# Attention inside a decoder layer: unscaled probabilities, and one multiplication of each value output by reciprocal row sums that travel through DRAM

## The chip, the cores and the metric

The kernel runs on one core of one Trainium2 chip. The metric is the device time of one execution in microseconds (us); the kernel before has a median of 2579.94 us over three runs (2579.6, 2579.94 and 2585.3 us).

A core has five engines with a queue each, and every queue is worked off in order: PE (matrix products, with PEld for its weight loads), DVE (vector work), ACT (activations and casts), POOL (vector work that can't reach PSUM) and SP, which here only issues DMA transfers. An instruction waits on semaphores of other engines or of DMA transfers, and all that stands behind it on its queue waits with it.

## The reference, cut to what matters

One decoder layer on a sequence of 2048 positions and 1024 channels: a projection, three groups of mixing heads beside each other (mLSTM, attention, spatial gating), an output projection, and a feed-forward part with a convolution. The change is in the attention: 8 heads of 64 channels, causal, with a cumulated log-forget bias `F`.

```python
def forgetting_attention(q, k, v, f_pre):
    F = jnp.cumsum(jax.nn.log_sigmoid(f_pre.astype(jnp.float32)), axis=-1)
    ...
        logits = (jnp.einsum('bhtd,bhsd->bhts', qb, kb) * scale
                  + F[:, :, lo:hi, None] - F[:, :, None, :hi])
        logits = jnp.where(mask, logits, -jnp.inf)
        p = jax.nn.softmax(logits, axis=-1)
        outs.append(jnp.einsum('bhts,bhsd->bhtd', p.astype(v.dtype), vb))
```

The softmax divides each row of exponentials by its sum. The product with the values is linear in the row, so the division can stand on the probabilities or on the output.

## The kernel before, in words

**Stages.** From 0 to about 700 us the kernel computes the projection, the mLSTM and the gating; from 700 to 1117 us the attention (the first two blocks of scores of head 0 run ahead, from 660 us); then the output projection, and from about 1290 us the feed-forward part.

**Tiling of the attention.** A phase is a head `h` and a block `tb` of 512 queries, written (h, tb) below. The order of the phases is (0,1), (0,0), (0,2), (0,3), then tb = 0, 1, 2, 3 for each of the heads 1 to 6, and 2, 3, 0, 1 for head 7 (`TBS`). `scores` makes the phase's four rows of 128 queries: `q` (split in two parts that sit above each other) times `kk` into PSUM tile `sp` (line 206, the mask by line 210), DVE adds the bias `nf`, finds the row minimum `nm` and writes `L` to SBUF (line 212), ACT takes the exponential in place and sums the row into `rs` (line 223). Then POOL adds the two partial sums where a row has two parts of up to 1024 keys (line 225), takes the power -1 (line 226), and multiplies the row in place by it (line 228).

`finish` takes the phase's rows one phase later: for each block `j` of 128 keys PE transposes the four row pieces into `tp` (line 259), ACT casts them to `phi` (line 262), DVE makes the rest `plo` (line 263), and PE multiplies both with the values `vv` into `op` (lines 245 and 246). `op` is a single PSUM buffer. After the last `j`, ACT copies it to `yo` (line 250), and two DMAs write the halves of `yo` to `yt_d` and `y2_d` in DRAM (line 252).

`phase` interleaves the scores of one block with the finish of the block before. `load_q` (line 173) fetches the queries a phase ahead into four buffers, `load_k` (lines 157 and 158) and `load_v` (line 163) the next head's keys, bias and values.

**What follows.** During the last two heads `load_w` fetches the output weights into three `ld` buffers and splits them (ACT line 131, POOL or DVE line 132), and `y_load` (lines 298 and 302) reads `yt_d` and `y2_d` back. The first block of the output projection is tb = 2. The casts of what was read (`yhl`, line 131) stand on ACT between the casts of the attention. The output products are lines 54 to 56 on `wps`.

**What sets the order.** Outside a few stretches written out by hand, a list scheduler with a cost model orders each queue and assigns buffers; the program order is its priority. All DMAs of this part are issued from SP.

Of the kernel before, what the change touches and what calls it, by code (L numbers as in the profile page):

```python
# [8 lines left out]
F32 = mybir.dt.float32  # L9
F32R = mybir.dt.float32r  # L10
BF16 = mybir.dt.bfloat16
AF = mybir.ActivationFunctionType
ALU = mybir.AluOpType
# [4 lines left out]
P = 128  # L18
S = 2048
D = 1024  # L20
DFF = 2816
NH = 8
EPS = 1e-6
NEG = -1.0e30
TB = 512
# [8 lines left out]
def trunk(  # L34
# [7 lines left out]
    V, A, G, T = nc.vector, nc.scalar, nc.gpsimd, nc.tensor  # L42
    dma = nc.sync.dma_start
# [15 lines left out]
    dr = ctx.enter_context(tc.tile_pool(name="dr", bufs=1, space=DRAM))  # L59
# [13 lines left out]
    gt_d = dr.tile([2, D], F32, name="gt_d")  # L73
    hc_d = dr.tile([7, 4, P, 2, 512], F32, name="hc_d")
    act_d = dr.tile([DFF, S], F32, name="act_d")


    ident = cst.tile([P, P], F32, name="ident")
# [3 lines left out]
    mone = cst.tile([P, 1], F32, name="mone")  # L82
# [42 lines left out]
    pool, pp = Mem(), Mem(PSUM)  # L125
# [10 lines left out]


    def attention_open_right():
        pool.open("att_s", "right", ("nm", 8, 6), ("rs", 8, 6), ("even", 128, 1))
        pool.open("att_r", "right", ("kvA", 8192, 3), ("LA", 4096, 8), ("qA", 2048, 6))  # L140
        pp.open("att_r", "right", ("sp", 4096, 2))

    def attention_open_left():
        pool.open(
            "att_l", "left", ("kvB", 8192, 6), ("LB", 4096, 12), ("L2", 2048, 4), ("phl", 2048, 8), ("qB", 2048, 4), ("yo", 2048, 2),
        )
        pp.open("att_l", "left", ("tp", 2048, 3), ("op", 2048, 1))

# [33 lines left out]
    def l_tile(h, tb, c, w):  # L182
        if h and (tb == 0 or (tb, c) == (2, 1)) or (h, tb, c) == (0, 2, 1):
            tag = "L2"
        else:
            n_l[0] += 1
            tag = "LA" if h < NH - 2 and (n_l[0] - 1) % 20 < 8 else "LB"
        return pool.tile([P, w], F32, name="L", tag=tag)

    def scores(h, tb, q2, rows):  # L190

        kk, nf, _ = kv[h]
        for i in range(4):
            n_s = (tb * 4 + i + 1) * P
            parts = [(s0, min(1024, n_s - s0)) for s0 in range(0, n_s, 1024)]
            qs = slice(i * P, (i + 1) * P)

            nm = pool.tile([P, 2], F32, name="nm", tag="nm")
            L = []
            for c, (s0, w) in enumerate(parts):  # L200
                sp = pp.tile([P, 1024], F32, name="sp", tag="sp")
                for b in range(0, w, 512):
                    bw = min(512, w - b)
                    last = s0 + b + bw == n_s
                    for n in range(2):
                        T.matmul(  # L206
                            sp[:, b : b + bw], q2[n][:, qs], kk[:, s0 + b : s0 + b + bw], start=n == 0, stop=n == 1 and not last
                        )
                    if last:
                        T.matmul(sp[:, w - P : w], identb, maskb, start=False, stop=True)  # L210
                L.append(l_tile(h, tb, c, w))
                V.tensor_tensor_reduce(  # L212
                    out=L[c], in0=sp[:, :w], in1=nf[:, s0 : s0 + w], scale=-1.0, scalar=3.0e38 if c == 0 else nm[:, 0:1],
                    op0=ALU.add, op1=ALU.min, accum_out=nm[:, c : c + 1],
                )
                yield
            rows.append(L)
            rs = pool.tile([P, 2], F32, name="rs", tag="rs")

            def exps(L=L, nm=nm, rs=rs):  # L220
                n = len(L)
                for c in range(n):
                    A.activation(L[c], L[c], AF.Exp, bias=nm[:, n - 1 : n], scale=-1.0, accum_out=rs[:, c : c + 1])  # L223
                if n == 2:
                    G.tensor_tensor(rs[:, 0:1], rs[:, 0:1], rs[:, 1:2], op=ALU.add)
                G.tensor_tensor(rs[:, 0:1], rs[:, 0:1], mone, op=ALU.pow)
                for t in L:
                    G.tensor_scalar(t, t, rs[:, 0:1], 1.0, op0=ALU.mult, op1=ALU.mult)  # L228

            exps()  # L230

    behind = []

    def finish(h, tb, rows):

        ns = (tb + 1) * 4
        vv = kv[h][2]

        got = []

        def product(j, c0, hi, lo):
            if j == 0:
                got.append(pp.tile([P, 512], F32, name="op", tag="op"))
            op = got[0]
            T.matmul(op[:, c0:], vv[:, j, :], hi[:, c0:], start=(j == 0), stop=False)  # L245
            T.matmul(op[:, c0:], vv[:, j, :], lo[:, c0:], start=False, stop=(j == ns - 1))  # L246
            if j == ns - 1:
                yo = pool.tile([P, 512], F32, name="yo", tag="yo")

                A.copy(yo, op)  # L250
                for n, d in enumerate((yt_d, y2_d)):
                    dma(d[h * 64 : h * 64 + 64, tb * TB : (tb + 1) * TB], yo[64 * n : 64 * n + 64])

        for j in range(ns):
            i0 = max(0, j - tb * 4)
            c0 = i0 * P
            tp = pp.tile([P, 512], F32, name="tp", tag="tp")
            for i in range(i0, 4):
                T.transpose(tp[:, i * P : (i + 1) * P], rows[i][j // 8][:, (j % 8) * P : (j % 8 + 1) * P], ident)  # L259
            hi = pool.tile([P, 512], F32R, name="phi", tag="phl")  # L260
            lo = pool.tile([P, 512], F32R, name="plo", tag="phl")
            A.copy(hi[:, c0:], tp[:, c0:])  # L262
            V.tensor_tensor(lo[:, c0:], tp[:, c0:], hi[:, c0:].bitcast(F32), op=ALU.subtract)  # L263
            behind.append(lambda j=j, c0=c0, hi=hi, lo=lo: product(j, c0, hi, lo))
            if len(behind) > 3:
                behind.pop(0)()
            yield

    def phase(now, then, lead=0):

        rows = []
        sc, n_sc = iter(()), 0
        if now:
            sc, n_sc = scores(*now, kv.pop(now) if now in kv else load_q(*now, "qB"), rows), (4, 4, 8, 8)[now[1]]
            if now in order and now != order[-1]:
                nxt = order[order.index(now) + 1]
                kv[nxt] = load_q(*nxt, "qB")
        n_fin = sum(4 * (t[1] + 1) for t in then)
        fin = (u for t in then for u in finish(*t))
        done = 0  # L280
        for n in range(n_sc):
            next(sc)
            while done < (n + 1 - lead) * (n_fin - 5) // (n_sc - lead):
                next(fin)
                done += 1
        for _ in sc:
            pass
        for _ in fin:
            pass
        return now and [(*now, rows)]  # L290
# [985 lines left out]
    for n, (half, i) in enumerate(steps):  # L1276
# [5 lines left out]
        if n == len(steps) - 1:  # L1282
            while background:
                if next(background[0], True):
                    background.pop(0)
            n_accs[0] = 2
            pool.close("proj_r")
            pp.close("proj_r")
            attention_open_right()

            load_k(0)
            first_rows = [], []
            first = [scores(0, tb, load_q(0, tb, "qA"), r) for tb, r in zip((1, 0), first_rows)]
            load_v(0, (0, 1))
            background += first
# [25 lines left out]
    for f in first:  # L1321
        for _ in f:
            pass
    attention_open_left()
    load_v(0, (2, 3))
    last = [(0, 1, first_rows[0]), (0, 0, first_rows[1])]
# [742 lines left out]
```

## Time and profile before

| | us |
|---|---|
| median of three runs | 2579.94 |
| the profiled execution | 2583.37 |
| its span in the trace | 2581.6 |
| attention, 701 to 1117 us | 416 |
| PE busy in it | 404.25 |
| DVE, ACT, POOL busy in it | 357.00, 338.90, 245.12 |
| matmul clock granted, mean of the span | 0.997 |

The views are those of one profiled execution. A group row names line, engine, operation, out<-in with shapes and the count, then busy us and mean ns of one, then the idle time before these instructions and what ended it. A row of waits names who waited for whom, the total in us, the number of times and the longest. A row of a timeline has the start, the length, the engine, the line and the operation; neighbours of one kind are merged, so the length of an "x4" row holds all four and the waits between them. Idle time of an engine that is not the bottleneck costs nothing, and a busy PE is not a PE at its peak, since its products are pipelined.

### The profile page before, as it was taken

How to read it: one execution, taken by the hardware profiler on the slowest of the kernel's cores; microseconds unless marked ns; L12 is line 12 of the kernel's file. 1: busy time of each engine (PE TensorE's matmuls, PEld its weight loads, DVE VectorE, ACT ScalarE, POOL GpSimd, SP SyncE). 2: the span in 40 equal slices, each digit the busy share in tenths (PEclk: the TensorE clock that was granted, in tenths of full speed). 3: DMA queues.
4: the chain of work that ended last, by engine and by line, in shares of the span. 5: the costliest groups of instructions: out<-in, count | busy, mean ns of one | idle time of the engine just before them, and what ended most of it. 6: DMA issues, size and time to landing. Idle time of an engine off the chain costs nothing.

```text
span 2581.6 us, 36385 instructions
## 1 busy us (share of the span) xinstructions
PE 2531.6 (98%) x12569; PEld 2099.5 (81%) x12569; DVE 1994.3 (77%) x3406; ACT 1282.8 (50%) x2443; POOL 405.2 (16%) x537
## 2 busy tenths in 40 slices
PE   7999999999999999999999999999999999999999
PEld 6888888888787877778878888888888888788787
DVE  7667656576388889865689888888888887897797
ACT  5433353433388888844455454444444444444443
POOL 2013310133266556510000000000000000000000
PEclk9999999999999999999999999999999999999999
DMA  7335753454654445266823222264222218567523
GB/s 260 116 119 168 222 173 101 133 160 139 177 158 128 123 127 168 56 200 230 285 82 106 84 80 83 89 233 158 82 82 86 78 67 293 178 207 249 188 90 123
DMA packets 302672, 379.58 MB, mean 147 GB/s; under 512 B 31758, under 2 KB 194412, under 8 KB 300440
## 3 DMA queue, kind: packets, MB, share of 16 engines
q1 hardware_dynamic: 302488, 377.26, 46.5%
q8 instruction: 99, 1.62, 0.3%
q14 instruction: 85, 0.70, 0.1%
HBM read 276.44 MB, written 100.74 MB: 146 GB/s over the span
## 4 chain that ended last, share of the span: by engine, by line
PE 49%; DVE 9%; DMA 5%; ACT 3%; issue 2%; POOL 1%; SPq 0%; DVEq 0%; ACTq 0%; POOLq 0%
PE ub L55 10%; PE ub L54 10%; PE ub L56 10%; PE db L55 3%; PE db L56 3%; PE db L54 3%; DVE wspl L1668 2%; PE tp L259 2%; PE sp L206 2%; DMA wd<-in_w_down_dram 2%; PE op L245 1%; PE op L246 1%; ACT L L223 1%; DVE L L212 1%; DMA hc_d<-hl 1%
## 5 line engine op out<-in xcount | busy, mean ns | idle before, releaser
L54 PE MATMUL acc<-wh,hh 128*128 128x512 f32 (+2 forms) x752 | 281.7, 375 | 1.2 <-DVE vhl L815 1.2
L54 PE MATMUL ub<-T,wsph 128*128 128x512 f32 x704 | 273.9, 389 | 1.2 <-ACT wsph L1529 1.2
L55 PE MATMUL ub<-T,wsph 128*128 128x512 f32 x704 | 274.3, 390 | 0.2 <-DVE T L1477 0.2
L56 PE MATMUL ub<-T,wspl 128*128 128x512 f32 x704 | 273.9, 389 | 0.0
L55 PE MATMUL acc<-wl,hh 128*128 128x512 f32 (+2 forms) x752 | 270.5, 361 | 0.6 <-DVE wl L648 0.6
L56 PE MATMUL acc<-wh,hl 128*128 128x512 f32 (+2 forms) x752 | 270.7, 362 | 0.3 <-DVE hl L606 0.2
L55 PE MATMUL db<-wspl,wsph 128*128 128x512 f32 x616 | 241.5, 392 | 4.4 <-DVE wspl L1668 4.1
L56 PE MATMUL db<-wsph,wspl 128*128 128x512 f32 x616 | 239.8, 389 | 0.0
L54 PE MATMUL db<-wsph 128*128 128x512 f32 x616 | 239.7, 389 | 0.0
L1529 ACT CAST wsph<-S 128x512 fp32r<-128x512 f32 x176 | 109.3, 622 | 219.5 <-PE ub L55 152.0
L263 DVE TENSOR_TENSOR plo<-tp,phi 128x512 fp32r<-128x512 f32 (+1 forms) x320 | 187.1, 607 | 30.7 <-ACT phi L262 28.5
L55 PE MATMUL ub<-B,wsph 128*128 128x512 f32 x528 | 205.7, 390 | 1.0 <-DVE B L1477 0.9
L54 PE MATMUL ub<-B,wsph 128*128 128x512 f32 x528 | 205.7, 390 | 0.0
L56 PE MATMUL ub<-B,wspl 128*128 128x512 f32 x528 | 205.4, 389 | 0.0
L223 ACT ACTIVATE L<-L,nm 128x1024 f32<-128x1024 f32 (+2 forms) x192 | 172.5, 903 | 34.5 <-DVE nm L212 32.7
L259 PE MATMUL tp<-ident,L 128*128 128x128 f32 x1088 | 177.3, 274 | 4.7 <-DVE plo L263 2.3
L262 ACT CAST phi<-tp 128x512 fp32r<-128x512 f32 (+1 forms) x320 | 160.0, 521 | 42.0 <-PE tp L259 40.3
L1667 ACT CAST wsph<-act 128x512 fp32r<-128x512 f32 x132 | 82.3, 624 | 195.7 <-PE db L55 187.9
L206 PE MATMUL sp<-kk,q 128*128 128x512 f32 (+3 forms) x640 | 169.3, 375 | 3.3 <-DVE nm L212 2.2
L228 POOL TENSOR_SCALAR L<-L,rs 128x1024 f32<-128x1024 f32 (+2 forms) x192 | 167.7, 884 | 11.0
L56 PEld LDWEIGHTS acc<-wh,hl 128*128 128x128 f32 x752 | 143.1, 191 | 22.4 <-DVE hl L606 0.9
L55 PEld LDWEIGHTS acc<-wl,hh 128*128 128x128 f32 x752 | 143.7, 191 | 20.5 <-DVE wl L648 1.8
(339 smaller groups left out, 5975.0 us busy)
## 6 DMA issues: line engine op xcount, KB each, us to landing
w<-in_w_up_dram SPq DMA_DIRECT2D x88, 512.0 KB
wd<-in_w_down_dram SPq DMA_DIRECT2D x176, 256.0 KB
wa<-in_w_ada_dram SPq DMA_DIRECT2D x96, 256.0 KB
act_d<-yc SPq DMA_DIRECT2D x44, 512.0 KB
act<-act_d SPq DMA_DIRECT2D x44, 512.0 KB
wr<-in_w_in_dram SPq DMA_DIRECT2D x64, 256.0 KB
q<-q_d SPq DMA_DIRECT2D x128, 128.0 KB
hc_d<-hl SPq DMA_DIRECT2D x28, 512.0 KB
```

The lines of the kernel that those rows point to most:

```text
L54: T.matmul(ps, lh, rh, start=start, stop=False, skip_group_check=resume)
L55: T.matmul(ps, lh, rl, start=False, stop=False, skip_group_check=resume)
L56: T.matmul(ps, ll, rh, start=False, stop=stop, skip_group_check=resume)
L206: T.matmul(sp[:, b : b + bw], q2[n][:, qs], kk[:, s0 + b : s0 + b + bw], start=n == 0, stop=n == 1 and not last)
L223: A.activation(L[c], L[c], AF.Exp, bias=nm[:, n - 1 : n], scale=-1.0, accum_out=rs[:, c : c + 1])
L228: G.tensor_scalar(t, t, rs[:, 0:1], 1.0, op0=ALU.mult, op1=ALU.mult)
L259: T.transpose(tp[:, i * P : (i + 1) * P], rows[i][j // 8][:, (j % 8) * P : (j % 8 + 1) * P], ident)
L262: A.copy(hi[:, c0:], tp[:, c0:])
L263: V.tensor_tensor(lo[:, c0:], tp[:, c0:], hi[:, c0:].bitcast(F32), op=ALU.subtract)
L1529: A.copy(self.wa[p][0], self.source(p))
L1667: A.copy(hi, v)
L1668: V.tensor_tensor(lo, v, hi.bitcast(F32), op=ALU.subtract)
```

## The change

The exponentials are no longer multiplied by POOL. The row sums of a phase's four rows go into one tile `rs` of 128 x 2 x 4; after the fourth row POOL adds the two halves and takes the power -1 for the four rows at once, and a DMA writes the 512 reciprocals, element by element, to a row of a new DRAM tensor `r_d`. When the phase's `op` has been copied to `yo`, a DMA reads that row back into all 128 partitions (`rb`, in the ring of `yo`, which now has four buffers), POOL multiplies `yo` by it, and only then the two halves are written. `rs` has five buffers of 32 bytes where it had six of 8, and an unused tile shrinks by as much, so that later addresses stay the same.

```diff
+    r_d = dr.tile([NH, S], F32, name="r_d")
...
-        pool.open("att_s", "right", ("nm", 8, 6), ("rs", 8, 6), ("even", 128, 1))
+        pool.open("att_s", "right", ("nm", 8, 6), ("rs", 32, 5), ("even", 16, 1))
...
-            ... ("qB", 2048, 4), ("yo", 2048, 2),
+            ... ("qB", 2048, 4), ("yo", 2048, 4),
...
     def scores(h, tb, q2, rows):
         kk, nf, _ = kv[h]
+        rs = pool.tile([P, 2, 4], F32, name="rs", tag="rs")
...
             rows.append(L)
-            rs = pool.tile([P, 2], F32, name="rs", tag="rs")
-
-            def exps(L=L, nm=nm, rs=rs):
-                n = len(L)
-                for c in range(n):
-                    A.activation(L[c], L[c], AF.Exp, bias=nm[:, n - 1 : n], scale=-1.0, accum_out=rs[:, c : c + 1])
-                if n == 2:
-                    G.tensor_tensor(rs[:, 0:1], rs[:, 0:1], rs[:, 1:2], op=ALU.add)
-                G.tensor_tensor(rs[:, 0:1], rs[:, 0:1], mone, op=ALU.pow)
-                for t in L:
-                    G.tensor_scalar(t, t, rs[:, 0:1], 1.0, op0=ALU.mult, op1=ALU.mult)
-
-            exps()
+            n = len(L)
+            for c in range(n):
+                A.activation(L[c], L[c], AF.Exp, bias=nm[:, n - 1 : n], scale=-1.0, accum_out=rs[:, c, i : i + 1])
+        if n == 2:
+            G.tensor_tensor(rs[:, 0, :], rs[:, 0, :], rs[:, 1, :], op=ALU.add)
+        G.tensor_tensor(rs[:, 0, :], rs[:, 0, :], mone.broadcast_to([P, 4]), op=ALU.pow)
+        dma(r_d[h, tb * TB : (tb + 1) * TB].rearrange("(i p) -> p i", p=P), rs[:, 0, :])
...
                 A.copy(yo, op)
+                rb = pool.tile([P, 512], F32, name="rb", tag="yo")
+                dma(rb, r_d[h : h + 1, tb * TB : (tb + 1) * TB].broadcast_to([P, TB]))
+                G.tensor_tensor(yo, yo, rb, op=ALU.mult)
                 for n, d in enumerate((yt_d, y2_d)):
                     dma(d[h * 64 : h * 64 + 64, tb * TB : (tb + 1) * TB], yo[64 * n : 64 * n + 64])
```

The scheduler orders the queues anew. Line numbers in the rows of the change are those of the changed kernel.

POOL's queue at head 1, in the kernel before: the end of the phase with tb = 1 and the start of the one with tb = 2 (`rs` the sums, `mone` the constant -1).

```order
L226 TENSOR_TENSOR rs<-rs,mone 128x1
L228 TENSOR_SCALAR L<-L,rs 128x896
L226 TENSOR_TENSOR rs<-rs,mone 128x1
L228 TENSOR_SCALAR L<-L,rs 128x1024
L225 TENSOR_TENSOR rs<-rs 128x1
L226 TENSOR_TENSOR rs<-rs,mone 128x1
L228 TENSOR_SCALAR L<-L,rs 128x1024
```

The same queue in the changed kernel, a whole head:

```order
L249 TENSOR_TENSOR yo<-yo,rb 128x512
L225 TENSOR_TENSOR rs<-rs,mone 128x4
L249 TENSOR_TENSOR yo<-yo,rb 128x512 x2
L224 TENSOR_TENSOR rs<-rs 128x4
L225 TENSOR_TENSOR rs<-rs,mone 128x4
L249 TENSOR_TENSOR yo<-yo,rb 128x512
L224 TENSOR_TENSOR rs<-rs 128x4
L225 TENSOR_TENSOR rs<-rs,mone 128x4 x2
```

A row's multiplications are gone, and four rows share one power. On PE the order stays as it was from phase (1,2) to the start of head 6 (some 17 of the 32 phases); it moves in small pieces before and after.

SP's queue at the start of the attention, before: the outputs of (0,1) and (0,0), and between and behind them the queries of (1,0) and (1,1).

```order
L252 DMA yt_d<-yo 64x512
L252 DMA y_d<-yo 64x512
L163 DMA vv<-v_d 128x4x128 x2
L173 DMA q<-q_d 64x512 x4
L252 DMA yt_d<-yo 64x512
L252 DMA y_d<-yo 64x512
L157 DMA kk<-k_d 64x2048
L173 DMA q<-q_d 64x512 x4
```

The same place in the changed kernel, from the store of (0,2)'s sums to that of (0,3)'s and the query part behind it:

```order
L226 DMA r_d<-rs 128x4x1
L164 DMA vv<-v_d 128x4x128
L248 DMA rb<-r_d 128x512
L164 DMA vv<-v_d 128x4x128 x3
L251 DMA yt_d<-yo 64x512
L251 DMA y_d<-yo 64x512
L174 DMA q<-q_d 64x512 x4
L248 DMA rb<-r_d 128x512
L158 DMA kk<-k_d 64x2048
L251 DMA yt_d<-yo 64x512
L251 DMA y_d<-yo 64x512
L174 DMA q<-q_d 64x512 x3
L226 DMA r_d<-rs 128x4x1
L174 DMA q<-q_d 64x512
```

The queries of (1,1) stood behind the write of (0,0); now three of their four parts also stand behind the load of `rb` for (0,0), and the fourth behind the store of (0,3)'s sums.

SP's queue near the end of the attention, before: the write of (7,2) and the reading back of block tb = 2 for the output projection.

```order
L252 DMA yt_d<-yo 64x512
L252 DMA y_d<-yo 64x512
L298 DMA ld<-yt_d 128x512
L302 DMA ld<-y_d 128x512
L298 DMA ld<-yt_d 128x512 x5
```

In the changed kernel, there:

```order
L226 DMA r_d<-rs 128x4x1 x2
L248 DMA rb<-r_d 128x512
L251 DMA yt_d<-yo 64x512
L251 DMA y_d<-yo 64x512
L297 DMA ld<-yt_d 128x512
L301 DMA ld<-y_d 128x512
L297 DMA ld<-yt_d 128x512 x5
```

The load of `rb` for (7,2) now stands behind the stores of two later phases' sums, (7,3) and (7,0), and in front of the write that the reading back waits for.

ACT's queue at that time, in phase (7,1), before: the casts of the attention (`phi`) and those of the blocks read back (`yhl`).

```order
L223 ACTIVATE L,rs<-L,nm 128x640
L262 CAST phi<-tp 128x512 x6
L131 CAST yhl<-ld 128x512
L262 CAST phi<-tp 128x512
L131 CAST yhl<-ld 128x512
L262 CAST phi<-tp 128x512 x2
L131 CAST yhl<-ld 128x512
```

In the changed kernel:

```order
L222 ACTIVATE L,rs<-L,nm 128x640
L261 CAST phi<-tp 128x512 x9
L132 CAST yhl<-ld 128x512
L261 CAST phi<-tp 128x384
L132 CAST yhl<-ld 128x512
L261 CAST phi<-tp 128x256
L261 CAST phi<-tp 128x128
L132 CAST yhl<-ld 128x512
```

The first cast of a block read back stands behind nine casts of the attention where it stood behind six, and the next ones follow it closer.

2 lines of the change are left out of this document (1 added, 1 removed).

## The prediction

> **What bounds the kernel now.** I read the page's busy times first, then the attention alone in the windows view, since every edit lies there.
>
> ```profile
> PE 2531.6 (98%) x12569; PEld 2099.5 (81%) x12569; DVE 1994.3 (77%) x3406; ACT 1282.8 (50%) x2443; POOL 405.2 (16%) x537
> 701.00:1117.00 416.00, 404.25 (x2473) 327.27 (x2472) 357.00 (x708) 338.90 (x737) 245.12 (x372) 1.00 0.47 128
> ```
>
> The second row lists PE, PEld, DVE, ACT and POOL busy, then the granted clock. In the 416 us of attention PE is busy for 404.25 us, at a clock of 1.00. It idles for 11.75 us, and POOL's 245.12 us lie beside that. Then the waits of PE and of its weight loader in the same stretch:
>
> ```profile
> PE op L245 <- ACT yo L250: 4.3, 13, 0.8
> PE tp L259 <- DVE plo L263: 2.3, 5, 0.7
> PE tp L259 <- POOL L L228: 1.2, 2, 1.0
> PEld tp L259 <- POOL L L228: 3.9, 8, 1.2
> PEld tp L259 <- POOL rs L226: 1.1, 1, 1.1
> ```
>
> PE's largest named wait is for the one `op` buffer, which the change leaves as it is. POOL ends 1.2 us of PE's idle time in 2 places and 5.0 us of the loader's in 9. The loader works ahead of PE, so part of its 5.0 us costs nothing. Last, the chain of waits over the attention, by line (the row ends there):
>
> ```profile
> by line: PE tp L259 11.4%; PE sp L206 10.5%; PE op L245 7.2%; issue 6.7%; PE op L246 6.5%; ACT L L223 4.6%; DVE L L212 4.6%; POOL L L228 3.3%; DVE plo L263 3.2%; ACT phi L262 2.8%; POOL rs L226 1.7%; DMA ld<-in_w_out_dram 1.4%; DMA ld<-yt_d
> ```
>
> POOL has 3.3% and 1.7%, thus 20.8 us of 416. This counts every step at which POOL came last before something, also where PE had other products meanwhile; the waits of PE itself are the better price, and the chain's share is kept for a rival.
>
> **What is taken out.** POOL's groups in the attention:
>
> ```profile
> L228 POOL TENSOR_SCALAR L<-L,rs 128x1024 f32<-128x1024 f32 (+4 forms) x184 | 161.8, 890 | 10.4
> L226 POOL TENSOR_TENSOR rs<-rs,mone 128x1 f32<-128x1 f32 x120 | 66.5, 557 | 77.6 <-ACT L L223 72.6
> L225 POOL TENSOR_TENSOR rs<-rs 128x1 f32<-128x1 f32 x64 | 13.5, 211 | 94.4 <-ACT L L223 94.3
> L132 POOL TENSOR_TENSOR wo0l<-ld,wo0h 128x512 fp32r<-128x512 f32 x4 | 5.2, 1290 | 6.9 <-ACT wo0h L131 6.9
> ```
>
> The multiplications go (161.8 us), and of the powers and sums three in four: 30 of the 120 powers stay (16.7 us), 16 of the 64 sums (3.4 us), if four columns cost what one does. New on POOL are 32 multiplications of 128x512; the last row is the same operation at the same size, 1.29 us, thus 41.3 us. POOL's 241.8 us fall to about 61 us. None of this is path by itself. ACT's exponentials and DVE's rows keep their number and size. What PE gains is that a row is ready after ACT instead of after ACT and POOL. The price is between 1.2 us (PE's idle time alone) and 6.2 us (the loader's too). I take 3.5, near the middle, since the loader's longest waits stand where PE waits too:
>
> ```profile
> 1107.63 0.33 PE L259 MATMUL tp<-ident,L 128*128 128x128 f32 x1 [0.97 <-POOL L L228]
> 1109.36 0.33 PE L259 MATMUL tp<-ident,L 128*128 128x128 f32 x1 [0.23 <-POOL L L228]
> ```
>
> These two are all of PE's 1.2 us, in the last phase. In the middle heads PE's order is unchanged, so nothing is to be had there but such waits.
>
> POOL also splits half of the first output weights, between its row multiplications. One wait there falls on ACT, which is on the path of the casts:
>
> ```profile
> ACT wo0h L131 <- DMA ld<-in_w_out_dram: 2.3, 2, 2.1
> ```
>
> A freer POOL gives the `ld` buffers back sooner. Between 0 and 2.3 us; I take 1, since the wait is ACT's and not PE's.
>
> **What is added, on the queues.** 64 DMAs (a store and a load in each phase) on SP, which has room. What counts is what stands behind their waits. A load that waits for a store of this part shows what a pass through DRAM takes:
>
> ```profile
> 1087.37 0.46 SPq L252 DMA_DIRECT2D yt_d<-yo  x1
> 1087.88 0.59 SPq L252 DMA_DIRECT2D y_d<-yo  x1
> 1089.68 0.33 SPq L298 DMA_DIRECT2D ld<-yt_d  x1
> 1090.33 0.33 SPq L302 DMA_DIRECT2D ld<-y_d  x1
> ```
>
> From the issue of `y_d` to that of its reader 2.45 us; I take 2.4 for a landing. The write of `yo` now waits for `rb` (2.4) and POOL (1.29), wherever `rb` is not early.
>
> Middle heads: the store of (h,1)'s sums and the loads of `rb` for (h,0) and (h,1) stand ahead of the queries of (h+1,0). Head 3 in the trace of before:
>
> ```profile
> 857.53 0.55 POOL L226 TENSOR_TENSOR rs<-rs,mone 128x1 f32<-128x1 f32 x1
> 865.82 2.46 SPq L173 DMA_DIRECT2D q<-q_d  x4
> 883.40 0.33 PE L206 MATMUL sp<-kk,q 128*128 128x128 f32 x2
> ```
>
> The sums of (3,1) are ready at 858.1, and the queries fetched at 865.8 are first used at 883.4. From the store on: landing x, `rb` 2.4, POOL 1.29, two writes 1.06, the last query part 0.59 and 1.8 to land, together 7.1 + x. This reaches 883.4 only if x is over 18 us. With x near 2.4 it costs 0; the cover is the 15 us by which the queries are early.
>
> Start: here the cover is thin. Queries of (1,1):
>
> ```profile
> 719.24 2.43 SPq L173 DMA_DIRECT2D q<-q_d  x4
> 726.08 2.46 SPq L173 DMA_DIRECT2D q<-q_d  x4
> 730.68 0.55 POOL L226 TENSOR_TENSOR rs<-rs,mone 128x1 f32<-128x1 f32 x1
> 733.21 0.69 PE L206 MATMUL sp<-kk,q 128*128 128x512 f32 x3
> ```
>
> They were issued at 726.1 and used at 733.2. Now the fourth part stands behind the store of (0,3)'s sums, whose power ends at 731.2: store 0.35, part 0.59, landing 1.8, so 734 against 733.2. I take 1 us of loss, between 0 (PE finds other products) and 2.
>
> End: `rb` of (7,2) stands behind the store of (7,0)'s sums. In before, their last power is here:
>
> ```profile
> 1087.02 0.55 POOL L226 TENSOR_TENSOR rs<-rs,mone 128x1 f32<-128x1 f32 x1
> 1095.62 0.62 ACT L131 CAST yhl<-ld 128x512 fp32r<-128x512 f32 x1 [1.69 <-DMA ld<-yt_d]
> 1098.45 0.62 ACT L131 CAST yhl<-ld 128x512 fp32r<-128x512 f32 x1 [0.23 <-DMA ld<-yt_d]
> 1100.23 0.62 ACT L131 CAST yhl<-ld 128x512 fp32r<-128x512 f32 x1 [0.51 <-DMA ld<-yt_d]
> ```
>
> Without the multiplications between, that power ends at about 1087.0; store 0.35, `rb` 0.4 after it, landing at 1089.7, POOL until 1091.0, the write 3.7 us later than at 1087.4. So the reading back is 3.7 us later, and ACT, which waited 1.69 us there, stands before it after three more casts of some 0.8 us (2.4 us). That leaves 1.69 + 3.7 - 2.4 = 3.0, which is 1.3 more, and the next two waits grow since fewer casts lie between: 2.5 us in all, between 0 (the output products already between the attention's fill PE) and 6.2 (3.7 and 2.5).
>
> **The sum.** -3.5 - 1 + 1 + 2.5 = -1 us. The bounds are -6.2 - 2.3 = -8.5 and -1.2 + 2 + 6.2 = +7. Against the profiled execution (2583.37, of which 1.8 lie outside its span) this is 2582.4. The median of the runs, 2579.94, lies 3.4 below that execution, so the forecast for the median is 2579, and from 2571.4 to 2587 by the bounds. 0.3% of 2580 is 7.7 us, about what a measurement of this kernel can tell from no change; nearly all of this lies inside it.
>
> **The rivals.** First, **slower, by the store of the sums**. It writes 512 separate elements of 4 bytes, and no row of before has such a store. Nearest is a load in 1024 pieces of 64 bytes:
>
> ```profile
> 15.45 0.39 SPq L1086 DMA_DIRECT2D gw<-in_w_in_dram  x1
> 20.79 0.58 POOL L1159 COPY wr<-gw 128x16 f32<-128x16 f32 x2 [5.98 <-DMA gw<-in_w_in_dram]
> ```
>
> 5.3 us from issue to use, which is under the 18 us of the middle heads. Above 18 us it decides: then SP stands before the write of (h,1), and the queries of each next head come late by what is over. At 20 us that is 2 us for each of 7 heads, +14, so 2593. For it: the path has four steps in series on one in-order queue, and nothing measures the first. Against it: a load of twice as many pieces takes 5.3. The Trainium skill speaks for this rival: "DMA: Bandwidth & Descriptors", section Rules for kernel authors, says that an access whose last dimension is not contiguous becomes one descriptor per element, and its Specifications say that under 512 bytes the engine reads, modifies and writes. No run shown here has a 4-byte store; by that rule x lies above a full-size landing, by how much the page doesn't say.
>
> Second, **faster, by the chain**. If each of POOL's steps in the chain is PE's own time, 20.8 us go instead of 3.5, which with the other terms gives -18.3, so 2562. For it: DVE and ACT are 86% and 81% busy here, so a row that is ready earlier may also spare waits that carry another engine's name. Against it: PE idles for 11.75 us in all, and only 1.2 of them end on POOL.
>
> **How the numbers follow.** No measurable change 0.54, the slow store 0.27, the chain 0.19. The predicted time is 2579. The likeliest case's own range is 2571 to 2587; cases of both signs hold nearly half, so the range goes on to 2566 and 2597, leaving out the farther half of the chain's gain and a store beyond 20 us. Faster by over 0.3% 0.19, within 0.54, slower 0.27.
>
> **What would show it.** Right: in 701 to 1117 us POOL's busy time near 65 us, no wait of `tp` for POOL, PE busy for some 404 us in a stretch as long as before; a short wait of PE near the first scores of (1,1); longer waits of ACT's `yhl` casts for `ld` between 1093 and 1105 us. Wrong: SP waiting at the write of `yo` past the time when queries are due, in every head; PE waiting for `sp`'s queries in the middle heads; or PE's waits for DVE and ACT falling by many us, which the orders don't explain.

## The result, and the profile after

The changed kernel takes 2710.34 us (median of four runs, 2704.91 to 2716.79) against 2579.77 of the kernel before on the same chip: a ratio of 1.0501, 95% interval 1.0489 to 1.0513. It is slower by 5%, some 130 us, where 2579 was forecast and 2597 was the upper end of the range.

Busy times of the page of the changed kernel, then its attention in the windows view (it now ends near 1231 us; PE, PEld, DVE, ACT and POOL busy, granted clock, DMA share, GB/s):

```profile
PE 2574.9 (95%) x12553; PEld 2123.1 (78%) x12569; DVE 1992.7 (73%) x3406; ACT 1285.1 (47%) x2443; POOL 231.5 (9%) x233
701.00:1231.00 530.00, 437.26 (x2499) 353.46 (x2499) 355.51 (x706) 341.48 (x737) 78.18 (x81) 0.91 0.53 115
```

POOL's work in the attention fell from 245 to 78 us, as the change means it to. But for about the same number of products (2499, before 2473) the stretch is 530 us long instead of 416. PE is idle for 93 us of it, where it was idle for 12, and busy for 33 us more, since the granted clock is 0.91 where it was 1.00. The waits of PE and of SP from 701 to 1250 us (total, times, longest):

```profile
PE sp L208 <- DMA q<-q_d: 46.4, 19, 7.0
PE tp L258 <- DVE plo L262: 23.2, 3, 8.6
PE sp L208 <- DVE nm L214: 20.2, 6, 9.7
...
SPq L251 <- POOL yo L249: 176.4, 20, 11.3
SPq L251 <- POOL rs L224: 63.1, 11, 10.5
SPq L226 <- POOL rs L225: 40.7, 14, 5.2
```

PE's largest wait is one that it did not have: for the queries. SP, which fetches them, stands for some 240 us before the writes of `yo` (line 251), because POOL's multiplication is not done. In the kernel before it stood there for 147 us (701 to 1117 us, for ACT), and no query was late for it. Why POOL is late shows in one stretch of a middle head, first SP's and POOL's queues, then PE's:

```profile
922.82 0.59 SPq L248 DMA_DIRECT2D rb<-r_d  x1
930.07 0.53 SPq L226 DMA_DIRECT2D r_d<-rs  x1
930.64 1.56 SPq L248 DMA_DIRECT2D rb<-r_d  x1
940.37 0.45 SPq L251 DMA_DIRECT2D yt_d<-yo  x1
941.56 2.47 SPq L174 DMA_DIRECT2D q<-q_d  x4
...
926.91 1.28 POOL L249 TENSOR_TENSOR yo<-yo,rb 128x512 f32<-128x512 f32 x1 [5.27 <-DMA rb<-r_d]
939.06 1.29 POOL L249 TENSOR_TENSOR yo<-yo,rb 128x512 f32<-128x512 f32 x1 [9.62 <-DMA rb<-r_d]
...
945.43 0.77 PE L208 MATMUL sp<-kk,q 128*128 128x512 f32 x1 [3.85 <-DMA q<-q_d]
```

The load of `rb` issued at 922.82, with no store just ahead of it, is there for POOL 4.1 us later. The one issued at 930.64, right behind a store of the sums, is there after 8.4. SP can't write before that, and only then fetches the queries, at 941.56; PE runs out of other work at that moment. For the most part the queries themselves are not slow here (median 3.6 us from issue to landing in this stage, upper quartile 4.9; 3.2 and 3.8 before): they are issued late. The same stretch in the windows view (columns as above):

```profile
936.00:941.00 5.00, 4.94 (x32) 3.65 (x30) 3.67 (x11) 4.69 (x12) 1.86 (x3) 1.00 0.00 0
941.00:945.00 4.00, 0.59 (x4) 0.21 (x2) 1.83 (x7) 1.02 (x4) 0.59 (x1) 0.86 0.63 161
945.00:950.00 5.00, 2.86 (x10) 2.24 (x11) 0.00 (x0) 0.28 (x1) 0.00 (x0) 0.50 1.07 219
952.00:957.00 5.00, 4.88 (x33) 4.05 (x32) 4.25 (x8) 4.00 (x9) 0.10 (x1) 1.00 0.84 143
```

After PE's gap the granted clock is 0.50 for several us, and a product of 128x512 with the queries takes 0.77 us (945.43, above) where a like one takes 0.40 at a clock of 1.00:

```profile
954.11 0.40 PE L208 MATMUL sp<-kk,q 128*128 128x512 f32 x1
```

So the wait costs more than its own length. The Trainium skill, "TensorE: Matmul & The Clock Gate", section Part 1: The HAM clock gate, says that the clock goes to half after an idle window of about 3.4 us. Here less was enough: by the trace's clock records it fell at 943.9 us, 2.3 us into this gap, and it also fell behind gaps of 1.9 and 2.1 us (before 781.98 and 843.66 us). The measurement decides.

### The profile page after: what moved, and what is told of

Its sections match the earlier page's. It is cut to its first block, busy times and chain, and to the rows that moved or that the text cites. A ratio compares the mean times of both kernels' runs of the same rounds, so it can differ in the third digit from the quotient of the medians.

```text
span 2715.1 us, 36025 instructions
## 1 busy us (share of the span) xinstructions
PE 2574.9 (95%) x12553; PEld 2123.1 (78%) x12569; DVE 1992.7 (73%) x3406; ACT 1285.1 (47%) x2443; POOL 231.5 (9%) x233
## 5 line engine op out<-in xcount | busy, mean ns | idle before, releaser
L54 PE MATMUL ub<-T,wsph 128*128 128x512 f32 x704 | 277.0, 394 | 1.2 <-ACT wsph L1528 1.2
L55 PE MATMUL ub<-T,wsph 128*128 128x512 f32 x704 | 277.3, 394 | 0.2 <-DVE T L1476 0.2
L208 PE MATMUL sp<-kk,q 128*128 128x512 f32 (+3 forms) x640 | 181.8, 396 | 69.3 <-DMA q<-q_d 46.4
L258 PE MATMUL tp<-ident,L 128*128 128x128 f32 x1088 | 185.2, 286 | 23.4 <-DVE plo L262 23.2
L208 PEld LDWEIGHTS sp<-kk,q 128*128 128x128 f32 x640 | 119.7, 201 | 101.8 <-issue 34.4
L258 PEld LDWEIGHTS tp<-ident,L 128*128 128x128 f32 x1088 | 138.8, 148 | 52.0 <-DVE plo L262 18.2
L214 DVE CUSTOM_DVE_ANT_0 L<-sp,nf 128x1024 f32<-128x1024 f32 (+7 forms) x128 | 126.0, 987 | 57.4 <-PE sp L208 24.1
```

What stands on the lines that cost most here:

```text
L54: T.matmul(ps, lh, rh, start=start, stop=False, skip_group_check=resume)
L55: T.matmul(ps, lh, rl, start=False, stop=False, skip_group_check=resume)
L208: T.matmul(sp[:, b : b + bw], q2[n][:, qs], kk[:, s0 + b : s0 + b + bw], start=n == 0, stop=n == 1 and not last)
L214: V.tensor_tensor_reduce(out=L[c], in0=sp[:, :w], in1=nf[:, s0 : s0 + w], scale=-1.0, scalar=3.0e38 if c == 0 else nm[:, 0:1], op0=ALU.add ...
```

## The experiments

Each kernel was compared with the kernel before on the same chip, and ratios are to that. "Lag" below is how far a kernel's profiled execution stands behind that of the kernel before at the same DVE instruction, worked out by pairing the DVE rows of both traces. The profiled execution of before is itself 3.4 us over its median and lost most of that ahead of 737 us, so from there on a lag of -3 means no difference (`before_shift`, which alters no order and has its effect behind the attention, shows -3.0).

| us of the kernel before | 641 | 737 | 770 | 965 | 1032 | 1180 | 1295 | 2150 |
|---|---|---|---|---|---|---|---|---|
| the change | 1.9 | 20.5 | 30.6 | 69.6 | 92.1 | 123.4 | 122.0 | 135.6 |
| `neither`: no store, no load | 0.2 | -2.8 | -3.2 | -5.3 | -6.2 | -7.6 | -8.3 | 5.3 |
| `store_only` | 0.4 | 15.2 | 17.8 | 44.1 | 61.0 | 74.8 | 74.6 | 88.2 |
| `load_only` | 0.1 | 2.8 | 3.1 | 0.8 | 12.1 | 22.3 | 18.7 | 31.5 |
| `neither_addr`: the same, addresses kept | -0.6 | -2.2 | -2.7 | -4.7 | -3.9 | -5.2 | -7.8 | -9.3 |
| `before_shift`: before, addresses moved | -0.1 | -3.0 | -3.0 | -3.0 | -2.2 | -2.3 | -1.9 | 11.2 |
| `fix_poolq`: 16 bytes, POOL's queue | -0.9 | -2.8 | -3.2 | -5.5 | 1.6 | 23.9 | 18.0 | 17.0 |
| `hybrid`: the same in heads 0 to 4 | -0.9 | -1.2 | -1.6 | -3.8 | 4.9 | 5.8 | 6.1 | 5.1 |
| `early_sp`: 16 bytes, SP, early load | 0.5 | -0.2 | -0.7 | -3.0 | -1.2 | 0.5 | -0.8 | -1.4 |

**Which part costs it.** Four kernels take the change apart. `neither`, from the change:

```diff
-        dma(r_d[h, tb * TB : (tb + 1) * TB].rearrange("(i p) -> p i", p=P), rs[:, 0, :])
...
-                rb = pool.tile([P, 512], F32, name="rb", tag="yo")
-                dma(rb, r_d[h : h + 1, tb * TB : (tb + 1) * TB].broadcast_to([P, TB]))
-                G.tensor_tensor(yo, yo, rb, op=ALU.mult)
```

> Without the store of the sums, the load of rb and POOL's multiplication by it: the division by the row sums is left out, POOL's row multiplications stay away. My theory (the 130 us come from the round trip of the sums on SP's in-order queue): all of them are gone, 2580 within 8 us, PE idle some 12 us in the attention. Rival, POOL's row work was part of the path before: below 2570, down to 2562. Rival, the loss comes from the new order of PE, ACT and DVE that goes with the change: above 2650 still.

`store_only` takes out the last three of these lines and keeps the store.

> Only the store of the sums, nothing reads them (the multiplication of yo and the load of rb are left out, so the outputs stay undivided). My theory (the stores cost by what waits for them, the loads of rb behind them and SP behind those): 2580 to 2600, since no instruction on SP waits for a store and the queries have some 15 us to spare. Rival, 16384 elements of 4 bytes take the DMA engines or the DRAM from everything else: above 2650, queries late in every head all the same.

`load_only` takes out the store, keeps the three, and fills `r_d` once at the start:

```diff
+    dma(r_d.rearrange("h (a b) -> (h a) b", b=P), ones)
```

> The sums are not stored (r_d holds ones, written once at the start; the division is left out), rb is loaded and multiplied as in the change. My theory: rb lands some 2.5 to 4 us after its issue instead of 8 to 9, SP is held for some 5 us a phase instead of 10 to 12, and the queries are in time in most heads: 2585 to 2625. Rival, any round trip ahead of the write of yo on SP is enough: above 2650, with PE waiting for q in every head.

`store_16b`:

```diff
-        dma(r_d[h, tb * TB : (tb + 1) * TB].rearrange("(i p) -> p i", p=P), rs[:, 0, :])
+        dma(r_d[h, tb * TB : (tb + 1) * TB].rearrange("(p i) -> p i", p=P), rs[:, 0, :])
```

> As the change, but each partition writes its four reciprocals as one piece of 16 bytes, 128 pieces instead of 512 (the reciprocals reach the wrong queries). My theory, landing goes by the number of pieces: some 4 us instead of 8.5, and 2600 to 2640. Rival, the time is in something that a store of 128 partitions has whatever its pieces: landing 8 us or more and above 2680.

| run | median, us | ratio, 95% interval |
|---|---|---|
| `neither` | 2586.69 | 1.0025, 1.0016 to 1.0035 |
| `store_only` | 2671.55 | 1.0351, 1.0334 to 1.0369 |
| `load_only` | 2614.81 | 1.0129, 1.0114 to 1.0144 |
| `store_16b` | 2611.87 | 1.0119, 1.0104 to 1.0134 |

The DMAs, with the multiplication that waits for them, are the loss: without them 0.25% is left. `neither` alone does not clear the new order of the queues, for in it DVE and ACT work in the order of the kernel before (all but one of DVE's 3406 instructions). `store_16b` does: all queues work in the order of the change there (PE's as far as its records go, of which some are missing), and it is 98 us faster than the change. My expectation for the store alone was wrong, though. Nothing reads the sums in `store_only`, and still it costs 3.26 points over `neither`, 84 us; load and multiplication alone cost 1.04 points, 27 us, and both together 12 us more than their sum. Waits of PE, then of SP, in `store_only`:

```profile
PE sp L208 <- DMA q<-q_d: 36.1, 13, 7.2
PE sp L208 <- DVE nm L214: 10.4, 3, 10.0
...
SPq L174 <- DMA nf<-nf_d: 25.3, 5, 6.7
...
SPq L174 <- DMA kk<-k_d: 21.1, 7, 5.6
```

SP now stands for 46 us before the queries until other loads have landed, keys and bias, where it does so for 0.5 us in `store_far64` (below). So the store delays transfers that have nothing to do with it. With pieces of 16 bytes it costs nothing that can be measured over `load_only`, and the 12 us that come only with both are gone too.

**Where the 13 us of the feed-forward are from.** `neither` is 8.3 us ahead at 1295 us and 5.3 behind at 2150, in a stage that the change doesn't touch. The groups of one product there, first the kernel before, then `neither`, then `neither_addr` (below):

```profile
L54 PE MATMUL ub<-T,wsph 128*128 128x512 f32 x704 | 273.9, 389 | 1.2 <-ACT wsph L1529 1.2
...
L54 PE MATMUL ub<-T,wsph 128*128 128x512 f32 x701 | 275.8, 394 | 1.2 <-ACT wsph L1524 1.2
...
L54 PE MATMUL ub<-T,wsph 128*128 128x512 f32 x704 | 273.9, 389 | 1.2 <-ACT wsph L1524 1.2
```

Each product takes 394 ns instead of 389, with the same order on PE. What is said ahead of the prediction, that the unused tile shrinks so that later addresses stay the same, is not so: in the compiled programs the tiles behind it lie 128 bytes higher (the first `wsph` buffer at 155232 instead of 155104). Three kernels test that. `neither_addr` and `after_addr`, from `neither` and from the change:

```diff
-        pool.open("att_s", "right", ("nm", 8, 6), ("rs", 32, 5), ("even", 16, 1))
+        pool.open("att_s", "right", ("nm", 8, 6), ("rs", 32, 5), ("even", 160, 1))
```

and `before_shift`, from the kernel before:

```diff
-        pool.open("att_s", "right", ("nm", 8, 6), ("rs", 8, 6), ("even", 128, 1))
+        pool.open("att_s", "right", ("nm", 8, 6), ("rs", 8, 6))
```

> As the run without store, load and multiplication (2586.7), but with the unused tile at 160 bytes instead of 16, so that all tiles behind it lie at the addresses of the kernel before (in the change they lie 128 bytes higher). Theory: the 13 us that the feed-forward lost there, at the same order of products and a clock of 1.00, come from the addresses: 2574, from 2570 to 2578. Rival, they come from anything else that the change alters ahead of the feed-forward: 2587 again.

> The kernel before without its unused tile of 128 bytes, so that all tiles behind it lie 128 bytes higher, where the change has them. Theory of the addresses: 2592, from 2588 to 2597, lost between 1390 and 2150 us. Rival, the addresses don't matter: 2580.

> The change with its unused tile at 160 bytes, so that the tiles behind it lie at the addresses of the kernel before; nothing else. Theory, the addresses are a term of their own, some 13 us beside the DMAs: 2694 to 2701. Rival, they matter only where PE is never idle, or not here: 2706 and above.

| run | median, us | ratio, 95% interval |
|---|---|---|
| `neither_addr` | 2573.64 | 0.9967, 0.9955 to 0.9978 |
| `before_shift` | 2594.75 | 1.0047, 1.0032 to 1.0062 |
| `after_addr` | 2695.08 | 1.0443, 1.0429 to 1.0457 |

All three came as the theory had them. The addresses alone cost 12 us in the kernel before and 15 in `neither` and in the change. In 400 us of that stage (1600 to 2000 us) PE does 1759 products in `before` and `neither_addr`, 1729 in `neither` and `before_shift`, at 398.81 us busy in all four:

```profile
1600.00:2000.00 400.00, 398.81 (x1759) 329.71 (x1758) 334.64 (x440) 189.19 (x308) 0.00 (x0) 1.00 0.35 119
...
1600.00:2000.00 400.00, 398.81 (x1729) 324.10 (x1728) 329.31 (x433) 186.52 (x304) 0.00 (x0) 1.00 0.35 118
```

The first row is the kernel before, the second `before_shift`. A busy PE does not show this; only the count, or the mean of one product, does.

**Why a store that nobody waits for holds up the rest.** Five kernels, all from `store_only`. `store_only_poolq`:

```diff
-        dma(r_d[h, tb * TB : (tb + 1) * TB].rearrange("(i p) -> p i", p=P), rs[:, 0, :])
+        for i in (0, 2):
+            G.dma_start(
+                r_d[h, tb * TB + i * P : tb * TB + (i + 2) * P].rearrange("(i p) -> p i", p=P), rs[:, 0, i : i + 2]
+            )
```

> As the run with the store alone (2671.6; nothing reads the sums, the outputs stay undivided), but the same 512 elements of 4 bytes go out on POOL's own queue, as two DMAs of 256 (with the addresses of the change). Theory, the transfers behind a store wait in its queue: with a queue of its own the queries land some 3 us after their issue again, and the time is 2587 to 2600. Rival, the elements hold up the DMA engines themselves, whatever the queue: above 2645, queries 8 us and more to landing.

`store_only_256` stores `rs[:, 0, 0:2]` alone.

> As the run with the store alone (2671.6 with 512 elements a phase), but only two of the four columns are stored, 256 elements of 4 bytes (nothing reads them, the outputs stay undivided, addresses of the change). Theory, each element holds a DMA engine for about as long, and the spare time of the queries takes the first part of it: less than half of the 85 us above the run without stores, 2590 to 2625. Rival, a store costs by itself and not by its elements: above 2650.

`store_far64` (and `store_far512`, with 128 in place of 16):

```diff
-    r_d = dr.tile([NH, S], F32, name="r_d")
+    r_d = dr.tile([NH, S, 16], F32, name="r_d")
...
-        dma(r_d[h, tb * TB : (tb + 1) * TB].rearrange("(i p) -> p i", p=P), rs[:, 0, :])
+        dma(r_d[h, tb * TB : (tb + 1) * TB, 0].rearrange("(i p) -> p i", p=P), rs[:, 0, :])
```

> As the run with the store alone (2671.6; nothing reads the sums, the outputs stay undivided), 512 elements of 4 bytes a phase, but each 64 bytes from the next in DRAM. Theory, neighbours hold each other up (16 elements shared 64 bytes, in the half store too, in the 16-byte form 4): the store lands in 3 to 4 us and the time is 2587 to 2605. Rival, each small write holds its engine whatever lies beside it: landing 8 us and more, 2660 to 2680.

> The same with the elements 512 bytes apart. Theory, neighbours: if the stretch they share is longer than 64 bytes this one is faster than the run at 64 bytes, at best 2587 to 2605; if it is 64 bytes or less both are equal. Rival, each write by itself: 2660 to 2680 in both.

`store_8b`:

```diff
+        dma(
+            r_d[h, tb * TB : (tb + 1) * TB].rearrange("(j p i) -> p j i", p=P, i=2),
+            rs[:, 0, :].rearrange("p (j i) -> p j i", i=2),
+        )
```

> As the run with the store alone, but 256 pieces of 8 bytes a phase (nothing reads them), as many pieces as the run of 256 elements (2658.5), each twice as long. Theory, neighbours: 8 pieces share 64 bytes instead of 16, so about half of that run's cost, 2605 to 2635. Rival, a fixed price per piece: 2650 to 2665.

The landing times are from the issue of a transfer to the last of its landing events in the trace, in the attention: the median of the stores, and median and upper quartile of the queries.

| run | median, us | ratio, 95% interval | store | queries |
|---|---|---|---|---|
| `neither` | 2586.69 | 1.0025 | | 3.1, 3.6 |
| `store_only` | 2671.55 | 1.0351 | 10.5 | 4.4, 9.1 |
| `store_only_poolq` | 2827.75 | 1.0962, 1.0935 to 1.0989 | | 8.1, 9.8 |
| `store_only_256` | 2658.53 | 1.0292, 1.0276 to 1.0307 | 9.7 | 4.3, 7.6 |
| `store_far64` | 2590.76 | 1.0036, 1.0023 to 1.0049 | 2.6 | 3.3, 3.9 |
| `store_far512` | 2587.80 | 1.0028, 1.0017 to 1.0039 | 2.7 | 3.3, 4.1 |
| `store_8b` | 2592.40 | 1.0042, 1.0025 to 1.0059 | 4.5 | 3.5, 5.3 |

A queue of its own made it far worse, and the queries on SP's queue take 8.1 us to land, as the rival said: the store holds up transfers of another queue. But this is not all of the 156 us over `store_only`. Waits of PE, SP and POOL in `store_only_poolq`:

```profile
PE sp L208 <- DMA q<-q_d: 99.5, 14, 53.4
...
SPq L297 <- POOL rs L224: 61.8, 1, 61.8
...
POOL r_d L227 <- issue: 489.0, 58, 13.6
```

POOL itself stands for 489 us before its stores and runs behind. PE's longest wait, 53.4 us, is for queries that stood on SP's queue behind a fetch of the output weights, and this waited 61.8 us for POOL. So the time of this run is no price of the store; the 8.1 us are what it shows.

Half the elements cost nearly as much, so it is not a price per element. The same 512 elements of 4 bytes, 64 bytes apart, cost next to nothing, with all queues in the order of `store_only`: they are dear only beside each other. Pieces of 8 bytes lie beside each other too and are cheap, more so than I expected.

The trace's records of single DMA packets say when the time passes. In `store_only` nine in ten of a store's small packets have begun 2.6 us after its issue, and one keeps its DMA engine for 9 ns; but the last landing comes 7.4 us later (medians of the 32 stores, worked out from the packets between issue and landing). With the elements 64 bytes apart these are 1.5 and 1.1 us, at the same 9 ns. So the elements don't keep the engines busy one by one; the time passes behind the last of them, before they have landed.

What is shown, then: a store of 4-byte writes to adjacent words takes some 10 us to land and delays other transfers, and either distance or a piece of 8 bytes ends most of that. Where the writes wait stays open, and so does one thing that goes with the size of a piece: a stretch of 64 bytes in DRAM is filled from 16 partitions by pieces of 4 bytes, from 8 by pieces of 8 and from 4 by pieces of 16. No run tells whether the small piece or the number of partitions that meet in one stretch makes it dear.

**What a cheap store leaves.** Six kernels do the whole computation with pieces of 16 bytes and the addresses of before. POOL undoes the order in its multiplication; `fix_sp`, from the change with its tile of 160 bytes:

```diff
+        dma(r_d[h, tb * TB : (tb + 1) * TB].rearrange("(p i) -> p i", p=P), rs[:, 0, :])
...
+                y4 = yo.rearrange("d (i p) -> d i p", p=P)
+                G.tensor_tensor(y4, y4, rb.rearrange("d (p i) -> d i p", p=P), op=ALU.mult)
```

`fix_poolq` issues store, load and writes from POOL (`G.dma_start`), and `hybrid` does that for heads 0 to 4 and multiplies the rows as before from head 5 on.

> The whole computation: store as 128 pieces of 16 bytes, the order undone in POOL's multiplication (rb read with a stride), store, load of rb and writes of yo on POOL's queue, addresses of the kernel before. Theory: no instruction on SP waits for the round trip, so it comes near the run without division at those addresses: 2573 to 2586. Rival, POOL's queue costs as much as it saves (writes and loads late, the ring of yo full): above 2600.

> The whole computation as in the run on POOL's queue (store in 16-byte pieces, addresses of the kernel before), but with store, load of rb and writes on SP, as in the change. Theory, 16-byte pieces and the addresses are most of the change's loss, and what stays is the round trip ahead of the write: as the run with 16-byte pieces (2611.9) less the 13 us of the addresses, 2596 to 2602, near the run on POOL's queue. Rival, SP's in-order wait is the larger part and POOL's queue had saved it: above 2610.

> The whole computation, addresses of the kernel before: heads 0 to 4 as in the run on POOL's queue (which was 5.5 us ahead of the kernel before at 965 us and lost 23 us after that), heads 5 to 7 with POOL's row multiplications as before. Theory, the rest of the loss is in the last heads, where the outputs are read back at once: the lead is kept, 4 us faster than before within 3 (ratio 0.9973 to 0.9996). Rival, the lead can't be kept since heads 5 to 7 take their old waits and the change between the two ways costs some: equal or slower.

The other three load `rb` at the head of `finish`, ahead of the transposes: `early_sp` is otherwise `fix_sp`, `early_poolq` is `fix_poolq`, and `early_mix` has only the writes on POOL's queue.

```diff
         got = []
+        rb = pool.tile([P, 512], F32, name="rb", tag="yo")
+        dma(rb, r_d[h : h + 1, tb * TB : (tb + 1) * TB].broadcast_to([P, TB]))
```

> The whole computation: 16-byte pieces, addresses of the kernel before, all on SP, and the load of rb placed in the program before the first transpose of the phase's finish instead of behind the copy of yo. Theory, the late load is what the round trip still costs: 2574 to 2586. Rival, SP's order of waits (store behind power, write behind multiplication) costs it whatever the load does: 2593 to 2600, as with the late load.

> The same early load, with store, load and writes on POOL's queue. Theory, the late load: 2574 to 2586. Rival, POOL's queue works off in order, a load that waits for its store holds up the multiplication of the phase before, and the last heads stay late: 2597 to 2605.

> The same early load, store and load on SP, the writes on POOL's queue behind the multiplication, so that SP never waits for it. Theory: the best of the three, 2573 to 2582, not slower than the kernel before. Rival, the reading back at the end waits for the writes whatever their queue: 2590 and above.

| run | median, us | ratio, 95% interval |
|---|---|---|
| `fix_poolq` | 2601.96 | 1.0071, 1.0054 to 1.0088 |
| `fix_sp` | 2596.46 | 1.0059, 1.0046 to 1.0073 |
| `hybrid` | 2586.33 | 1.0021, 1.0012 to 1.0030 |
| `early_sp` | 2582.51 | 1.0016, 1.0007 to 1.0026 |
| `early_poolq` | 2586.64 | 1.0031, 1.0021 to 1.0040 |
| `early_mix` | 2584.12 | 1.0019, 1.0010 to 1.0029 |

The late load costs 11 us, the difference between `fix_sp` and `early_sp`; `early_sp` is still 13 us behind `neither_addr`, and the cause of these 13 was not isolated. Four expectations were missed: `fix_poolq` and `hybrid` came as their rivals had it, `early_poolq` lies just above its range, and `early_mix` is not the best of the three. Three of PE's waits from 700 to 1320 us, first in `fix_sp`, then in `early_sp`:

```profile
PE sp L208 <- DVE nm L214: 5.3, 4, 2.6
PE sp L208 <- DMA q<-q_d: 5.0, 3, 3.3
PE wps L54 <- ACT wo1h L132: 4.4, 1, 4.4
...
PE sp L208 <- DVE nm L214: 1.4, 5, 0.4
...
PE wps L54 <- ACT wo1h L132: 0.3, 1, 0.3
PE sp L208 <- DMA q<-q_d: 0.3, 1, 0.3
```

`fix_poolq` keeps its lead until 965 us and loses 29 us from there to 1180, in the last heads. `hybrid`, made to avoid that, loses 9 at its seam instead, where the rows of head 5 stand on POOL behind a multiplication that waits for `rb`:

```profile
965.35 1.58 POOL L264 TENSOR_TENSOR yo<-yo,rb 128x512 f32<-128x512 f32 x1 [5.85 <-DMA rb<-r_d]
975.40 0.47 PE L273 MATMUL tp<-ident,L 128*128 128x128 f32 x1 [2.13 <-POOL L L230]
```

None of the six beats the kernel before; the best is 0.16% behind it. What could be won at most is shown by `neither_addr`, which leaves the division out: 0.33%.

## Why the prediction was wrong

**What bounds the kernel** was read rightly: PE, which idled for 12 us in all. That also gave the right size of the gain. **The rows taken off POOL** were priced at -3.5 us, with -1 for the output weights; `neither_addr` gains 8.5 us (0.33%; 5.7 to 11.6), at the bound of -8.5. In its profile some 2 of them are gained in the attention to 1107 us (a lag of -4.3 against -2.2 at 737 us) and about 3 more by 1295; in `neither` 4 and 1.5. Both terms had the right sign and were somewhat small. The rival of the chain, 20.8 us, is refuted: POOL's share of the chain was no price. POOL's own work was put about 16 us too low, since a power of four columns takes 1.02 us and not the 0.56 of one; `neither_addr` has the same powers and is ahead all the same.

**The middle heads** were priced at 0 as long as a landing x is under 18 us. That step failed, and it is the main one. The medians of landing in the change are 10.2 us for the store and 9.1 for `rb`, well under 18, and yet the change loses 61 us between 770 and 1032 us of before, 12 in each head. With 10.2 in place of x and 9.1 in place of the 2.4 for `rb`, the path that the step added up takes 24 us and would still be inside the 25.3 us from 858.1 to 883.4, so it was the path that was wrong and not only its sizes. Two things were left out. The step asked who waits for the store, and priced that once for each head; but a store of adjacent 4-byte elements delays the transfers around it, which `store_only` shows with nothing reading the sums (84 us). And it took 2.4 us for `rb` from transfers of large rows; without any store around it is 4.5 (`load_only`), with the change's store 9.1 (the store in 16-byte pieces leaves it at 4.5), four times a head, each time with SP standing before the write. That these passes add up until the cover under the queries is gone fits PE's waits for queries in the middle heads, but no run isolates it.

Without the 4-byte store the step held for most of the middle heads: from 770 to 965 us the lag of `load_only` falls from 3.1 to 0.8. There the four passes of a head through SP cost nothing, as predicted. From 965 to 1032 us, where SP's queue also holds the fetches of the output weights, `load_only` loses 11 us and `neither` gains 1; the prediction has no term for that.

**The nearest row** for the store, a load in 1024 pieces of 64 bytes in 5.3 us, was the wrong neighbour: a load, of longer pieces. `store_far64` shows that 512 elements of 4 bytes can indeed land in 2.6 us, so the count did not mislead me, but that words of 4 bytes lie side by side.

**The slow store**, the rival with a chance of 0.27, names the right cause and the wrong price: 14 us, from what is over 18 us in each of 7 heads. The measured x would have given 0 by its rule. The Trainium skill, "DMA: Bandwidth & Descriptors", section Rules for kernel authors, warns of an access with one descriptor per element; the change bears that out, but by that rule `store_far64`, with as many elements, would be as slow, and it is not (2591 us), nor is it the size under 512 bytes, which all these stores have. The measurement decides. The same list says that DMAs issued from several engines run on the same 16 DMA engines, and the queries' 8.1 us in `store_only_poolq` agree.

**The start** was put at +1 and the change is 20.5 us behind at 737 us and 30.6 at 770; 9 of them lie ahead of 707 us, the first stores being issued from 671 us on. Of the load and the multiplication alone some 6 are due (`load_only` at 770 us, 3.1 against `neither`'s -3.2), 21 of the store alone (17.8 against -3.2), and some 7 come only with both. **The end**, +2.5 with an upper bound of 6.2, is 31 us between 1032 and 1180 us; 12 of them remain in `load_only` (10 against -1.4 in `neither`). In the change the mechanism was there, the reading back later than the casts, but the forecast looked at one load only: from 1030 to 1231 us DVE waits 26.2 us for `ld<-y_d` (2.2 in the kernel before, 965 to 1117), and PE waits 23.2 and 20.0 us for DVE and 0.2 for queries. In `load_only` it is not that: ACT waits for `ld<-yt_d` as long as before (4.9 us from 1044 to 1205 us, 4.7 in the kernel before from 1032 to 1185). What costs there is the last write: SP issues it after `rb` and POOL, and behind it stands `gt`, a factor of the output projection, for which DVE waits 11.7 us (4.7 before), and behind that PE waits once for the output weights:

```profile
PE wps L54 <- ACT wo1h L133: 8.8, 1, 8.8
```

In the change DVE waits 9.1 us for `gt`.

**What was not seen at all**: the addresses, +15 us, against my own statement that they stay; and the clock. PE is busy for 33 us more in the attention for 26 more products, which explain 4 of them at the old pace; the other 29 go with the clock, which falls behind such waits. A price of PE's idle time alone, as the sum made it, is too low here.

Taken together, in points of the time before: rows -0.33, addresses +0.58, store +3.26, load and multiplication +1.04, and 0.46 that the last two cost only together: 5.01. The first two and the next two are differences of measured ratios; the 0.46 is what is left. It needs the slow store, since `store_16b` is no slower than `load_only`; that it comes from SP's waits for loads that the store delays (rows 930 to 945 us) is argued. Seen from the change itself, pieces of 16 bytes alone take away 3.82 of the 5.01 points, 98 us.

## What to carry to other kernels

Price a DMA by what it does to all transfers in flight and not only by who waits for it, and look at how its elements lie: here 512 reciprocals a phase as 4-byte words side by side cost 84 us, and 98 with the load behind them; as 128 pieces of 16 bytes they cost nothing that could be measured. A load that closes a round trip belongs as early in the program as its data exist. And when a tile in front changes size, compare the addresses behind it, and the mean time of products in stages that the change doesn't touch.

## What the runs showed of the hardware that was not expected

- 4-byte writes to adjacent DRAM words land in 10.5 us a store (512 of them) or 9.7 (256), the same writes 64 bytes apart in 2.6, 8-byte pieces side by side in 4.5. The adjacent words hold up transfers of other queues as well: the queries took 8.1 us instead of 3.1 with the store on POOL's queue. Their packets take 9 ns each either way; the time passes between the last packet and the landing (7.4 us, 1.1 with the elements 64 bytes apart).
- Moving the tiles behind one unused tile by 128 bytes in SBUF made the products of the up projection 394 ns long instead of 389, at a clock of 1.00 and with the same order: 12 us in the kernel before (interval of the ratio 1.0032 to 1.0062), 15 in two others. Which address or access makes it was not tried.
- A gap of 4 us on PE was followed by a granted clock of 0.50 for several us, and so were gaps of 1.9 and 2.1 us; over the attention of the change the mean was 0.91, which cost some 29 us (an estimate, from 33 us more of busy time for 26 more products) beside the 81 of added idle time.
